# A decoder layer on one core: an eighth chunk of the last projection in seven products, with weight sums made in DRAM by accumulating DMAs

## The chip, the core and the metric

The kernel runs on one core of a Trainium2 chip. Time is the device time of one execution in microseconds (us); a profiled execution also has a span, from its first instruction to its last. Engines are TensorE (PE in the profile; PEld are its weight loads), VectorE (DVE), ScalarE (ACT), GpSimd (POOL) and SyncE (SP). Each runs its own queue in the order in which the program names its instructions, and waits at an instruction until what it needs is there. DMAs are issued from the queues of SP, ACT or POOL.

## What is computed

A decoder layer for 256 tokens of width 1024 in fp32: a mixer (causal pooling beside block attention), cross-attention into 256 memory tokens, and a SwiGLU FFN of width 2816, each followed by a residual and a LayerNorm. Only the last part matters here:

```python
def swiglu(h, w_gate, w_up, w_down):
    return (jax.nn.silu(h @ w_gate) * (h @ w_up)) @ w_down
...
h = layer_norm(DEEPNORM_ALPHA * h + swiglu(h, w_gate[l], w_up[l], w_down[l]), ln3_g[l], ln3_b[l])
```

## The kernel before

**Products in halves.** A product of fp32 matrices is made from halves of both operands, a high part cast to fp32r (ScalarE) and the rest, the low part (VectorE), as three matmuls: high times high, high times low, low times high (`three`, L359). So every weight tile, 128 partitions by 1024 numbers (0.524 MB), is loaded raw, cast by ScalarE, and its low part made by VectorE.

**The weights' stream.** The class `Stream` holds all weights in one list in the order of use. `fetch_ahead` (L112) issues the loads from SP, with up to 7 raw tiles not yet split (pool "raw", 7 buffers). `prepare` (L148) splits a tile; `next` (L176) splits one more whenever TensorE is done with one, and keeps 8, later 10, split tiles ahead (`widen`, L108). `before(number, load)` puts another load in front of a tile's load.

**Gate and up.** The FFN's width is cut into 11 chunks of 256 (c = 0 to 10), whose weights are tiles w59 to w102, four for each chunk. `h2T` is the transposed input, in two tiles of the pool "a8": k = 0 to 3 and k = 4 to 7. A pass of the loop at L997 runs chunk c through `proj_both` (L369): matmuls with high weights into four PSUM banks (L377), then with low weights (L383). The last three passes do this in groups of two k, a tile of weights at a time. Odd passes use the banks of `accbank`, even ones those of `bank`, four each. After a pass, `Gated.add` empties its banks (L963 ScalarE, L964 VectorE). In the next pass `multiply` (L968, L969) and `split` (L971) follow, after the pass's second and fourth step: the gated values are cast to high and low parts (L429, L430).

**Down.** The second product, with w_down, takes the chunks in the order `DOWN = (1, 2, 0, 3, ..., 10)`. A chunk multiplies a 256 x 256 block of gated values with a 256 x 1024 block of weights. Seen as 2 x 2 blocks that is eight products of 128 x 128 by 128 x 512, or seven with Strassen's scheme in Winograd's form: sums of quarters of both operands are multiplied, and the seven results are shared among the outputs. Chunks 1 to 7 (`SEVEN`) take seven products (`seven`, L1033), 21 matmuls; chunk 0 takes eight (`eight`, L1054), 24 matmuls; chunks 8, 9 and 10 (`LAST`) take eight too, ordered by output quarter (`pieces`, L1065), so that the last LayerNorm can begin on the first half. The products go to PSUM banks m1, m2, m3, m5 (`accbank`) and m7, m6, m4, m0 (`bank`). A chunk's first five products are in the order m1, m2, m3, m5, m7.

The sums of a seven-product chunk's weights are made on VectorE in `prepare_pair` (L122): four subtractions of 128 x 512 beside three low parts of 128 x 1024 and one of 128 x 512, in three steps for the chunk's three tiles. Those of its gated values are made in `split` (L977 to L984): four operations of 128 x 128 and a second cast and low part.

**Buffers of gated values.** A seven-product chunk takes a whole tile of the pool "a8" for its gated values and their sums (`gated_parts`, L912); of the others, the first two share one such tile (go0), the third takes two tiles of the pool "pr", the fourth half a tile of "a8". The pool "a8" has `A8_BUFS = 11` buffers (L33). A new tile of a pool takes over a buffer, and its first writer waits until the last reader of the buffer's former tile is done. `h2` (the residual, read at the end) and `h2T` are also tiles of "a8".

Of the kernel before, what the change touches and what calls it, by code (L numbers as in the profile page):

```python
# [23 lines left out]
FB = DFF // P  # L24
# [10 lines left out]
BUSY = 7  # L35


DOWN = (1, 2, 0, 3, 4, 5, 6, 7, 8, 9, 10)
SEVEN = (1, 2, 3, 4, 5, 6, 7)
LAST = DOWN[-3:]  # L40
ALL = slice(None)

# [3 lines left out]
def r32(t):  # L46
    return t.bitcast(F32)


class Stream:  # L50
# [71 lines left out]
    def prepare_pair(self, i, hi, lo):  # L122
        nc = self.nc
        first, step = self.pairs[i]
        self.fetch(first + 3, nc.sync)
        x, y, z = self.raws[first:first + 3]
        h = x.shape[2] // 2
        (x1, x2), (y1, y2), (z1, z2) = [(a[:, :, :h], a[:, :, h:]) for a in (x, y, z)]
        sub = nc.vector.tensor_sub

        if step == 0:
            own = self.corner[first] = self.own(first)
            nc.scalar.copy(own[:, 0:1, :], x1)
            nc.scalar.copy(hi, y)
            sub(z1, x2, x1)
            sub(z2, y2, x2)
            sub(own[:, 1:2, :], x1, r32(own[:, 0:1, :]))
            sub(x2, y2, z1)
            sub(lo, y, r32(hi))
        elif step == 1:  # L140
            nc.scalar.copy(hi, z)
            sub(x1, y1, x2)
            sub(lo, z, r32(hi))
        else:
            nc.scalar.copy(hi, x)
            sub(lo, x, r32(hi))
# [59 lines left out]
@with_exitstack  # L206
def decoder_layer(
    ctx: ExitStack, tc: tile.TileContext, x, x_t, mem_t, w_qkv, w_u, w_pool, w_out,
    ln1_g, ln1_b, w_xq, w_xk, w_xkv, w_xo, ln2_g, ln2_b, w_gu, w_down, ln3_g, ln3_b, out,
):  # L210
    nc = tc.nc
    cp = ctx.enter_context(tc.tile_pool(name="const", bufs=1))
# [20 lines left out]
    ws = Stream(nc, rp, wp)  # L233
# [5 lines left out]
    def rows(w, k0, c0, nk=1, width=D):  # L239
        return ws.add(w[k0 * P:(k0 + nk) * P, c0:c0 + width].rearrange("(k p) n -> p k n", p=P), 1)  # L240
# [20 lines left out]
    c_xq = [cols(w_xq, c) for c in range(4)]  # L261
    c_xo = [rows(w_xo, k, 0) for k in range(KD)]
    c_gu = [ws.add(w_gu[c], 4) for c in range(NFC)]
    c_dn = {}
    for c in DOWN:
        tiles = [w_down[k * P:(k + 1) * P, :].rearrange("(k p) n -> p k n", p=P) for k in (2 * c, 2 * c + 1)]
        c_dn[c] = ws.add_pair(*tiles) if c in SEVEN else [ws.add(w, 1)[0] for w in tiles]
    ws.own = lambda i: sp.tile([P, 2, 512], F32R, tag="pair", bufs=3, name=f"w{i}c")


# [1 line left out]
    class Both:  # L272
# [62 lines left out]
    ws.before(c_dn[LAST[0]][0], load_norm("g", 3, ln3_g))  # L335
    ws.before(c_dn[LAST[0]][1], load_norm("b", 3, ln3_b))

    ident = cp.tile([P, P], F32, name="ident")
    make_identity(nc, ident)
    ident_r = cp.tile([P, P], F32R, name="ident_r")  # L340
# [4 lines left out]
        out=tri[:, P:], in_=tri[:, P:], compare_op=OP.is_ge, fill=NEG, base=0,  # L345
# [6 lines left out]
    mhalf = cp.tile([P, 32], F32, name="mhalf")[:, 0:1]  # L352
# [16 lines left out]
    def proj_both(pss, numbers, yT, group=KD):  # L369

        for k0 in range(0, KD, group):
            for k in range(k0, k0 + group):
                hi, _ = ws.get(numbers, k)
                for b, ps in enumerate(pss):
                    nc.tensor.matmul(ps, hi[:, b * P:(b + 1) * P], yT.both(k), start=k == 0, stop=False,  # L377
                                     skip_group_check=True)
                yield
            for k in range(k0, k0 + group):  # L380
                _, lo = ws.parts_of(numbers, k)
                for b, ps in enumerate(pss):
                    nc.tensor.matmul(ps[:, S:], lo[:, b * P:(b + 1) * P], yT.pair(k)[0], start=False,  # L383
                                     stop=k == KD - 1, skip_group_check=True)
# [313 lines left out]
    class Norm:  # L698
# [9 lines left out]
        def add(self, c0, c1, acc):  # L708
            self.sum(c0, c1, acc)
            self.measure(c0, c1)  # L710
# [219 lines left out]
    def gated_pair(c, k, t):  # L930

        return pair(gT[c], ALL, 2 * k + t)
# [18 lines left out]
    class Gated:  # L951
# [19 lines left out]
        def split(self):  # L971
            gated_parts(self.c)
            hi, lo = gT[self.c]
            q = self.sums[0].rearrange("p f (t s) -> p (f t) s", t=T)
            split(hi[:, 0:4], lo[:, 0:4], q)
            if self.c in SEVEN:
                a11, a21, a12, a22 = [q[:, i] for i in range(4)]  # L977
                sums = sp.tile([P, 4, P], F32, name="sg", tag="pr", bufs=PR_BUFS)
                s1, s2, s3, s4 = [sums[:, i] for i in range(4)]
                nc.vector.tensor_add(s1, a21, a22)  # L980
                nc.vector.tensor_sub(s3, a11, a21)
                nc.vector.tensor_sub(s2, s1, a11)
                nc.vector.tensor_sub(s4, a12, s2)  # L983
                split(hi[:, 4:8], lo[:, 4:8], sums)  # L984

    first = [bank("pg") for t in range(T)]
# [37 lines left out]
    m = {n: accbank(f"m{n}") for n in (1, 2, 3, 5)}  # L1024
# [3 lines left out]
    def into(n, y, w, cols=ALL, ps=None):  # L1028

        three((m[n] if ps is None else ps)[:, cols], y, w, n not in begun, True, True)  # L1030
        begun.add(n)
# [17 lines left out]
            ws.used += 1  # L1049
            ws.next()  # L1050

    QUARTERS = {2: (0, 0, 512), 3: (0, 512, D), 4: (1, 0, 512), 0: (1, 512, D)}

    def eight(c):  # L1054

        for k, number in enumerate(c_dn[c]):
# [42 lines left out]
    lower, upper = slice(0, 512), slice(512, D)  # L1099
    norms = [Norm(3, t, h2[:, t, :]) for t in range(T)]  # L1100
# [10 lines left out]
    m1, u2, u3 = [shared_sum(name) for name in ("m1", "u2", "u3")]  # L1111
# [3 lines left out]
    with_residual(0, upper, m[5])  # L1115
    nc.vector.tensor_add(u3, m[7], u2)
    with_residual(1, upper, m[5])
    nc.vector.tensor_add(norms[0].r[:, upper], norms[0].r[:, upper], u2)
    nc.vector.tensor_add(norms[1].r[:, upper], norms[1].r[:, upper], u3)
# [15 lines left out]
    for half in HALVES:  # L1135
# [28 lines left out]


_INS = ["x", "x_t", "mem_t", "w_qkv", "w_u", "w_pool", "w_out", "ln1_g", "ln1_b", "w_xq", "w_xk",
        "w_xkv", "w_xo", "ln2_g", "ln2_b", "w_gu", "w_down", "ln3_g", "ln3_b"]


# [42 lines left out]
```

## Time and profile before

| | us |
|---|---|
| median of 3 runs | 377.5 (377.05 to 377.51) |
| the profiled execution | 376.66 |
| its span | 374.9 |
| TensorE busy | 368.5 |
| VectorE busy | 306.8 |
| ScalarE busy | 204.1 |
| GpSimd busy | 19.6 |

In a list of instructions in order of time, a line gives start, duration, engine, line of the kernel, operation, output and inputs with shapes, and in brackets how long the engine idled before it and what ended that. In a table by stretches, a line gives from:to, its length, then for PE, PEld, DVE, ACT and POOL the busy time and number of instructions, the TensorE clock that was granted (1.00 is full), the DMA engines' mean busy share, and GB/s. The chain of waits is the work that ended last, followed back from the end.

### The profile page before, as it was taken

The page shows a single profiled execution, that of the slowest core. Times are in us where ns is not written, and L with a number is a line of the kernel's source. Part 1 is how long each engine was busy: PE and PEld are TensorE (multiplying, and loading weights), DVE is VectorE, ACT ScalarE, POOL GpSimd, SP SyncE. Part 2 cuts the span into 40 slices and gives each one's busy share as a digit, 9 for nine tenths or more (in the row PEclk, how much of TensorE's full clock was granted, in tenths as well). Part 3 has the DMA queues.
Part 4 walks back from the last instruction along what each step waited for, and adds up shares of the span by engine and source line. Part 5 has one row for each costly group of instructions (what it writes and reads, how often), then busy time and mean ns, then how long its engine had stood idle before and what let it go on. Part 6 is the DMA issues. An engine that isn't in the chain of part 4 may idle for free.

```text
span 374.9 us, 5582 instructions
## 1 busy us (share of the span) xinstructions
PE 368.5 (98%) x2061; PEld 317.6 (85%) x2061; DVE 306.8 (82%) x498; ACT 204.1 (54%) x330; POOL 19.6 (5%) x27
## 2 busy tenths in 40 slices
PE   9999999999999999999999999999999999999994
PEld 8997878787888889998888888888898888888883
DVE  6768799975599677865889688888888999999984
ACT  6746677644154635644237675567665675546510
POOL 1000033400020000000100000000000000000021
PEclk9999999999999999999999999999999999999998
DMA  8997784668508963343106958665554453375202
GB/s 274 415 416 270 222 282 124 214 214 292 169 0 281 387 210 133 113 156 123 60 2 221 326 184 278 226 219 176 173 180 170 152 170 113 119 275 162 64 0 112
DMA packets 20891, 71.93 MB, mean 192 GB/s; under 512 B 2304, under 2 KB 3072, under 8 KB 20736
## 3 DMA queue, kind: packets, MB, share of 16 engines
q1 hardware_dynamic: 20432, 71.12, 54.3%
q10 hardware_dynamic: 432, 0.46, 0.4%
q8 instruction: 16, 0.26, 0.3%
q14 instruction: 11, 0.09, 0.1%
HBM read 70.52 MB, written 1.05 MB: 191 GB/s over the span
## 4 chain that ended last, share of the span: by engine, by line
PE 97%; DMA 1%; DVE 1%; ACT 0%; issue 0%; POOLq 0%; ACTq 0%
PE pg L377 19%; PE pg L383 10%; PE pqk L483 6%; PE m L362 5%; PE m L364 5%; PE m L363 5%; PE acc L362 4%; PE acc L363 4%; PE acc L364 4%; PE pxk L377 4%; PE pxq L377 4%; PE pxq L383 2%; PE pu L377 2%; PE pxk L383 2%; PE xv L362 2%; PE xv L364 2%
## 5 line engine op out<-in xcount | busy, mean ns | idle before, releaser
L725 POOL TENSOR_TENSOR rs<-rs,mhalf 128x1 f32<-128x1 f32 x6 | 5.0, 830 | 291.2 <-DVE rs L724 291.2
L429 ACT CAST g<-sg 128x512 fp32r<-128x512 f32 x14 | 8.7, 621 | 19.1 <-DVE sg L983 12.4
L430 DVE TENSOR_TENSOR g<-sg,g 128x512 fp32r<-128x512 f32 x14 | 9.7, 692 | 8.9 <-ACT g L429 8.9
L964 DVE TENSOR_TENSOR sg<-pg,sg 128x256 f32<-128x256 f32 x40 | 14.1, 416 | 0.0
L963 ACT COPY sg<-pg 128x256 f32<-128x256 f32 x40 | 11.8, 379 | 2.1 <-PE pg L383 2.1
L968 ACT ACTIVATE sg<-sg 128x512 f32<-128x512 f32 x10 | 6.3, 635 | 12.1 <-DVE sg L964 12.0
L520 ACT ACTIVATE xpr<-xs,mx 128x256 f32<-128x256 f32 x8 | 3.7, 470 | 14.3 <-DVE mx L531 14.3
L520 ACT ACTIVATE pr<-pr,mx 128x128 f32<-128x128 f32 (+1 forms) x16 | 7.1, 445 | 7.6 <-DVE mx L551 7.6
L429 ACT CAST h2T<-tp 128x512 fp32r<-128x512 f32 x4 | 2.3, 586 | 12.9 <-PE tp L440 12.9
L730 DVE SCALAR_TENSOR_TENSOR r<-r,mv,gb 128x512 f32<-128x512 f32 (+2 forms) x12 | 8.3, 722 | 0.0
L717 DVE BATCH_NORM_STATS2 st<-r 128x6 f32<-128x512 f32 (+1 forms) x12 | 8.0, 670 | 0.3
L969 DVE TENSOR_TENSOR sg<-sg 128x512 f32<-128x512 f32 x10 | 6.9, 692 | 0.8
L596 POOL TENSOR_TENSOR win<-upad 128x542 f32<-128x542 f32 x2 | 4.0, 1998 | 56.9 <-DVE upad L627 56.9
L525 DVE RECIPROCAL sm<-sm 128x2 f32<-128x2 f32 x12 | 2.0, 166 | 6.0 <-ACT xpr L520 4.5
L835 PE MATMUL xs<-xkTh,xq 128*128 128x256 f32 x32 | 6.4, 282 | 0.0
L429 ACT CAST h1T<-tp 128x512 fp32r<-128x512 f32 x4 | 2.4, 588 | 7.2 <-PE tp L440 7.2
L735 DVE SCALAR_TENSOR_TENSOR h<-r,rs,gb 128x512 f32<-128x512 f32 x8 | 5.7, 746 | 0.1
L596 POOL TENSOR_TENSOR win<-win 128x269 f32<-128x269 f32 (+3 forms) x4 | 5.8, 1446 | 0.2
L635 ACT CAST xkTh<-pxk 128x256 fp32r<-128x256 f32 x8 | 2.6, 377 | 5.5 <-PE pxk L383 5.5
L637 DVE TENSOR_TENSOR xkl<-pxk,xkTh 128x256 f32<-128x256 f32 x8 | 3.0, 416 | 3.1 <-ACT xkTh L635 3.1
L835 PEld LDWEIGHTS xs<-xkTh,xq 128*128 128x128 f32 x32 | 5.2, 190 | 0.2
L170 ACT CAST w39h<-w39r 128x1024 fp32r<-128x1024 f32 x1 | 1.0, 1049 | 7.8 <-PE acc L364 7.8
(1157 smaller groups left out, 1294.8 us busy)
## 6 DMA issues: line engine op xcount, KB each, us to landing
gb<-in_ln_g SPq DMA_DIRECT2D x3, 512.0 KB, 6.0
gb<-in_ln_b SPq DMA_DIRECT2D x3, 512.0 KB, 7.5
wr<-in_w_qkv SPq DMA_DIRECT2D x5, 256.0 KB, 4.4
mr<-in_mem_t SPq DMA_DIRECT2D x1, 1024.0 KB, 11.4
xt<-in_x SPq DMA_DIRECT2D x1, 1024.0 KB, 7.8
xr<-in_x_t SPq DMA_DIRECT2D x3, 256.0 KB, 6.1
wr<-in_w_qkv SPq DMA_DIRECT2D x1, 512.0 KB, 6.0
w7r<-in_w_qkv SPq DMA_DIRECT2D x1, 512.0 KB, 6.9
```

The lines of the kernel that those rows point to most:

```text
L362: nc.tensor.matmul(ps, wa, ya, start=start, stop=False, skip_group_check=part)
L363: nc.tensor.matmul(ps, wa, yb, start=False, stop=False, skip_group_check=part)
L364: nc.tensor.matmul(ps, wb, ya, start=False, stop=stop, skip_group_check=part)
L377: nc.tensor.matmul(ps, hi[:, b * P:(b + 1) * P], yT.both(k), start=k == 0, stop=False, skip_group_check=True)
L383: nc.tensor.matmul(ps[:, S:], lo[:, b * P:(b + 1) * P], yT.pair(k)[0], start=False, stop=k == KD - 1, skip_group_check=True)
L429: nc.scalar.copy(h, ps)
L483: nc.tensor.matmul(qk[i][:, f, :], w[:, c * P:(c + 1) * P], y, start=k == 0 and f == 0 and w is hi and y is x_hi, stop=k == KD - 1 and w i ...
L520: nc.scalar.activation(dst[:, j, :], src[:, j, :], AF.Exp, bias=mx[:, j:j + 1], scale=sign, accum_out=sm[:, j:j + 1])
L596: nc.gpsimd.tensor_add(nxt[:, j:, 2 * n - 1:], cur[:, j:, 2 * n - 1:], cur[:, j:, n - 1:PADW + S - n])
L835: nc.tensor.matmul(ps[:, t, :], q[:, kk, t * P:(t + 1) * P], k[:, 2 * h + kk], start=n == 0, stop=q is q_lo and kk == 1, skip_group_check= ...
L963: nc.scalar.copy(y[:, f, :], ps[:, S:])
L964: nc.vector.tensor_add(y[:, f, :], ps[:, :S], y[:, f, :])
```

## The change

Chunk 8 becomes the eighth chunk of seven products; chunk 0 takes its place among the last three, so that `eight` goes away and nothing is preloaded into m0. The scheme's signs are changed so that all sums of weights are additions. For chunks 5 to 8 (`SUMMED`) the sums are no longer made on VectorE. The host lays the quarters of these chunks' weights out as a further input, `w_sum` (order: lower left, lower right, upper right, upper left). Two DMAs on SP copy pairs of quarters to DRAM scratch tensors `sum_z` and `sum_w` (2.1 MB each) during the passes of cross-attention and gate, and three accumulating DMAs on POOL, named in pass 3 of gate and up, add further quarters to them (2.1, 2.1 and 1.05 MB). In down such a chunk loads tiles y (two plain quarters), z and w (two sums each) and, for two chunks at a time, o (their upper left quarters), 14 tiles for the four chunks, each split as a plain tile. Nothing changes in the pools but the padding of a constant; `dynamic_dma_scratch_size` goes from 256 to 1024.

```diff
-DOWN = (1, 2, 0, 3, 4, 5, 6, 7, 8, 9, 10)
-SEVEN = (1, 2, 3, 4, 5, 6, 7)
+DOWN = (1, 2, 3, 4, 5, 6, 7, 8, 0, 9, 10)
+SEVEN = DOWN[:-3]
+SUMMED = (5, 6, 7, 8)
 LAST = DOWN[-3:]
...
+    dram = ctx.enter_context(tc.tile_pool(name="dram", bufs=1, space=bass.MemoryType.DRAM))
+    sum_z, sum_w = [dram.tile([P, 2, len(SUMMED), 512], F32, name=f"sum_{name}") for name in "zw"]
     c_dn = {}
     for c in DOWN:
...
+        if c in SUMMED:
+            j = SUMMED.index(c)
+            order = [("y", w_sum[:, 0:2, j, :]), ("z", sum_z[:, :, j, :]), ("w", sum_w[:, :, j, :])]
+            if j % 2 == 0:
+                order.append(("o", w_sum[:, 3, j:j + 2, :]))
+            c_dn[c] = {what: ws.add(src, 1)[0] for what, src in order}
...
+    ws.before(c_gu[1][0], lambda: nc.sync.dma_start(sum_z, w_sum[:, 1:3]))
+    ws.before(c_gu[2][0], lambda: nc.sync.dma_start(sum_w, w_sum[:, 0:2]))
+
+    def add_quarters():
+        def add(dst, src):
+            nc.gpsimd.dma_start(dst, src, accum_op=OP.add, max_dma_last_dim=8192)
+
+        add(sum_z, w_sum[:, 2:4])
+        add(sum_w, sum_z[:, 1:2].to_broadcast(list(sum_w.shape)))
+        add(sum_w[:, 0], w_sum[:, 1])
...
         if c == 3:
             ws.widen(late)
+            add_quarters()
...
+    def summed(c):
+
+        plan = {"y": ((c, 2, 2), (c, 3, 7)), "z": ((c, 7, 6), (c, 5, 4)), "w": ((c, 4, 3), (c, 6, 5)),
+                "o": ((c, 1, 0), (c + 1, 1, 0))}
+        for what, number in c_dn[c].items():
             ws.prepare(number + 1)
-            hi, lo = ws.tiles[number]
-            for n, (t, c0, c1) in QUARTERS.items():
-                into(n, gated_pair(c, k, t), (hi[:, 0, c0:c1], lo[:, 0, c0:c1]))
+            for half, (of, n, form) in enumerate(plan[what]):
+                into(n, pair(gT[of], ALL, form), tuple(a[:, half] for a in ws.tiles[number]))
+                yield
             ws.used += 1
             ws.next()
-            yield
...
         for c in DOWN[:-len(LAST)]:
-            yield from (seven if c in SEVEN else eight)(c)
+            yield from (summed if c in SUMMED else seven)(c)
...
-    add(norms[1], 768, D, m[0][:, 256:])
```

More of the change, by code (lines that the diff above doesn't have):

```diff
@@ L128, in prepare_pair @@
         (x1, x2), (y1, y2), (z1, z2) = [(a[:, :, :h], a[:, :, h:]) for a in (x, y, z)]
-        sub = nc.vector.tensor_sub
+        sub, add = nc.vector.tensor_sub, nc.vector.tensor_add
         if step == 0:
@@ L134, in prepare_pair @@
             nc.scalar.copy(hi, y)
-            sub(z1, x2, x1)
-            sub(z2, y2, x2)
+            add(z1, x2, x1)
+            add(z2, y2, x2)
             sub(own[:, 1:2, :], x1, r32(own[:, 0:1, :]))
-            sub(x2, y2, z1)
+            add(x2, y2, z1)
             sub(lo, y, r32(hi))
@@ L141, in prepare_pair @@
             nc.scalar.copy(hi, z)
-            sub(x1, y1, x2)
+            add(x1, y1, x2)
             sub(lo, z, r32(hi))
@@ L208, in decoder_layer @@
     ctx: ExitStack, tc: tile.TileContext, x, x_t, mem_t, w_qkv, w_u, w_pool, w_out,
-    ln1_g, ln1_b, w_xq, w_xk, w_xkv, w_xo, ln2_g, ln2_b, w_gu, w_down, ln3_g, ln3_b, out,
+    ln1_g, ln1_b, w_xq, w_xk, w_xkv, w_xo, ln2_g, ln2_b, w_gu, w_down, w_sum, ln3_g, ln3_b, out,
 ):
@@ L266, in decoder_layer @@
         tiles = [w_down[k * P:(k + 1) * P, :].rearrange("(k p) n -> p k n", p=P) for k in (2 * c, 2 * c + 1)]
-        c_dn[c] = ws.add_pair(*tiles) if c in SEVEN else [ws.add(w, 1)[0] for w in tiles]
+        if c in SUMMED:
[4 more added lines that the diff above has]
+            c_dn[c] = {what: ws.add(src, 1)[0] for what, src in order}
+        elif c in SEVEN:
+            c_dn[c] = ws.add_pair(*tiles)
+        else:
+            c_dn[c] = [ws.add(w, 1)[0] for w in tiles]
     ws.own = lambda i: sp.tile([P, 2, 512], F32R, tag="pair", bufs=3, name=f"w{i}c")
@@ L350, in decoder_layer @@
                    allow_small_or_imprecise_dtypes=True)
-    mhalf = cp.tile([P, 32], F32, name="mhalf")[:, 0:1]
+    mhalf = cp.tile([P, 96], F32, name="mhalf")[:, 0:1]
     nc.vector.memset(mhalf, -0.5)
@@ L979, in split @@
                 s1, s2, s3, s4 = [sums[:, i] for i in range(4)]
-                nc.vector.tensor_add(s1, a21, a22)
+                nc.vector.tensor_sub(s1, a21, a22)
                 nc.vector.tensor_sub(s3, a11, a21)
                 nc.vector.tensor_sub(s2, s1, a11)
-                nc.vector.tensor_sub(s4, a12, s2)
+                nc.vector.tensor_add(s4, a12, s2)
                 split(hi[:, 4:8], lo[:, 4:8], sums)
@@ L1050, in seven @@
             ws.next()
-    QUARTERS = {2: (0, 0, 512), 3: (0, 512, D), 4: (1, 0, 512), 0: (1, 512, D)}
-    def eight(c):
-        for k, number in enumerate(c_dn[c]):
+    def summed(c):
+        plan = {"y": ((c, 2, 2), (c, 3, 7)), "z": ((c, 7, 6), (c, 5, 4)), "w": ((c, 4, 3), (c, 6, 5)),
+                "o": ((c, 1, 0), (c + 1, 1, 0))}
+        for what, number in c_dn[c].items():
             ws.prepare(number + 1)
-            hi, lo = ws.tiles[number]
-            for n, (t, c0, c1) in QUARTERS.items():
-                into(n, gated_pair(c, k, t), (hi[:, 0, c0:c1], lo[:, 0, c0:c1]))
+            for half, (of, n, form) in enumerate(plan[what]):
+                into(n, pair(gT[of], ALL, form), tuple(a[:, half] for a in ws.tiles[number]))
+                yield
             ws.used += 1
             ws.next()
-            yield
+    QUARTERS = {2: (0, 0, 512), 3: (0, 512, D), 4: (1, 0, 512), 0: (1, 512, D)}
     def pieces():
@@ L1117, in decoder_layer @@
     with_residual(1, upper, m[5])
-    nc.vector.tensor_add(norms[0].r[:, upper], norms[0].r[:, upper], u2)
-    nc.vector.tensor_add(norms[1].r[:, upper], norms[1].r[:, upper], u3)
+    nc.vector.tensor_sub(norms[0].r[:, upper], norms[0].r[:, upper], u2)
+    nc.vector.tensor_sub(norms[1].r[:, upper], norms[1].r[:, upper], u3)
     with_residual(1, lower, u3)
-    add(norms[1], 768, D, m[0][:, 256:])
     rest = [sp.tile([P, CW], F32R, name=f"rest{i}", tag="pr", bufs=PR_BUFS) for i in range(2)]
@@ L1166 @@
 _INS = ["x", "x_t", "mem_t", "w_qkv", "w_u", "w_pool", "w_out", "ln1_g", "ln1_b", "w_xq", "w_xk",
-        "w_xkv", "w_xo", "ln2_g", "ln2_b", "w_gu", "w_down", "ln3_g", "ln3_b"]
+        "w_xkv", "w_xo", "ln2_g", "ln2_b", "w_gu", "w_down", "w_sum", "ln3_g", "ln3_b"]
 def kernel(**inputs):
@@ L1173 @@
     from concourse.bass_utils import run_bass_kernel_spmd
-    nc = bacc.Bacc("TRN2", target_bir_lowering=False, num_devices=1, dynamic_dma_scratch_size=256)
+    nc = bacc.Bacc("TRN2", target_bir_lowering=False, num_devices=1, dynamic_dma_scratch_size=1024)
     arrays, args = {}, []
@@ L1202 @@
     given["w_gu"] = np.concatenate([chunks(given["w_gate"]), chunks(given["w_up"])], axis=3)
+    quarters = given["w_down"].reshape(FB // 2, 2, P, 2, 512)[list(SUMMED)]
+    given["w_sum"] = np.stack([quarters[:, i, :, j].transpose(1, 0, 2) for i, j in ((1, 0), (1, 1), (0, 1), (0, 0))],
+                              axis=1)
     for name in _INS:
```

## The prediction

> **What bounds the kernel now.** First the page's span and busy times, then the chain that ended last, cut out where gate and up give way to down.
>
> ```profile
> span 374.9 us, 5582 instructions
> PE 368.5 (98%) x2061; PEld 317.6 (85%) x2061; DVE 306.8 (82%) x498; ACT 204.1 (54%) x330; POOL 19.6 (5%) x27
> ```
>
> ```profile
> 306.89 1.84 PE pg L377 x8
> 311.52 0.95 PE pg L383 x8
> 312.48 0.23 PE m L362
> 316.81 0.23 PE m L363
> ```
>
> TensorE is the bound, and at 312.48 down's first product (into m, L362) follows gate and up's last matmul without a gap. Nineteen matmuls of 128x512 start between 312.48 and 316.81: 4.33 / 19 = 0.228 us each. A matmul removed is worth that, as long as nothing makes TensorE wait. So the next view is the busy time in stretches.
>
> ```profile
> 290.00:298.00 8.00, 8.00 (x48) 6.99 (x47) 7.72 (x13) 5.25 (x10) 0.00 (x0) 1.00 0.56 190
> 298.00:306.00 8.00, 8.00 (x47) 7.00 (x46) 7.94 (x13) 4.05 (x8) 0.00 (x0) 1.00 0.31 90
> 306.00:314.00 8.00, 8.00 (x48) 7.03 (x47) 7.72 (x12) 5.94 (x11) 0.00 (x0) 1.00 0.49 177
> ```
>
> After the stretch come length, PE, PEld, DVE, ACT, POOL. VectorE is busy 7.72, 7.94 and 7.72 of 8 us just before down. It hides behind TensorE, with nothing to spare: whatever holds it up here is passed on.
>
> **The change, part by part.**
>
> *Matmuls.* Chunk 8 goes from eight products to seven: 3 x 0.228 = 0.68 us less on the path. Chunk 0 takes its place in the last pieces, same matmuls.
>
> *Chunk 8's gated values.* SEVEN now holds 8, so gated_parts(8) takes a whole tile of the pool "a8". Count its 11 buffers when chunk 8 is split, in pass c = 9: h2T has two, h2 one, go0 one, g1 to g7 seven. All live: passes 9 and 10 still read h2T, the end reads h2, down the rest. In before, chunk 8 went into the second half of go0 and needed none. The twelfth tile must wait for the first of the eleven to be read out, which is h2T's first half (k = 0 to 3). Pass 10 reads it last at k = 3, that is with w100. ScalarE casts into the tile first, and its queue is in order:
>
> ```profile
> 295.43 1.03 ACT L145 CAST w105h<-w103r 128x1024 fp32r<-128x1024 f32 x1
> 296.37 0.61 ACT L429 CAST go<-sg 128x512 fp32r<-128x512 f32 x1
> 296.89 0.61 ACT L133 CAST w106c<-w106r 128x512 fp32r<-128x512 f32 x1
> ```
>
> ```profile
> 303.94 2.00 PE L377 MATMUL pg<-h2T,w100h 128*128 128x512 f32 x8
> 305.78 1.12 PE L383 MATMUL pg<-h2T,w100l 128*128 128x256 f32 x8
> 306.73 2.00 PE L377 MATMUL pg<-h2T,w101h 128*128 128x512 f32 x8
> ```
>
> The cast now at 296.37 (go, chunk 8) would wait until the w100 matmuls end at 306.9. TensorE gets there unhindered: weights up to w105 are cast ahead of it in the queue, and pass 10's banks are emptied at 294. Behind the waiting cast stand w106 and all later weights, and the emptying of passes 9's and 10's banks; VectorE stops at the low part that follows.
>
> ```profile
> 284.43 0.69 DVE L430 TENSOR_TENSOR g<-sg,g 128x512 fp32r<-128x512 f32 x1
> 285.03 0.29 DVE L980 TENSOR_TENSOR sg<-sg 128x128 f32<-128x128 f32 x1
> 286.73 0.69 DVE L430 TENSOR_TENSOR g<-sg,g 128x512 fp32r<-128x512 f32 x1 [0.69 <-ACT g L429]
> 292.37 0.69 DVE L142 TENSOR_TENSOR w103r<-w104r,w103r 128x512 f32<-128x512 f32 x1
> 294.11 1.41 DVE L964 TENSOR_TENSOR sg<-pg,sg 128x256 f32<-128x256 f32 x4
> 297.64 0.68 DVE L430 TENSOR_TENSOR go<-sg,go 128x512 fp32r<-128x512 f32 x1
> 298.24 0.69 DVE L135 TENSOR_TENSOR w108r<-w106r 128x512 f32<-128x512 f32 x1
> 303.66 1.22 DVE L146 TENSOR_TENSOR w108l<-w106r,w108h 128x1024 fp32r<-128x1024 f32 x1
> 304.81 1.41 DVE L964 TENSOR_TENSOR sg<-pg,sg 128x256 f32<-128x256 f32 x4
> 307.19 1.23 DVE L172 TENSOR_TENSOR w109l<-w109r,w109h 128x1024 fp32r<-128x1024 f32 x1 [0.18 <-ACT w109h L170]
> 308.33 0.69 DVE L430 TENSOR_TENSOR go<-sg,go 128x512 fp32r<-128x512 f32 x1
> 308.94 1.22 DVE L172 TENSOR_TENSOR w110l<-w110r,w110h 128x1024 fp32r<-128x1024 f32 x1
> 310.07 0.69 DVE L135 TENSOR_TENSOR w113r<-w111r 128x512 f32<-128x512 f32 x1
> 313.62 1.41 DVE L964 TENSOR_TENSOR sg<-pg,sg 128x256 f32<-128x256 f32 x4
> ```
>
> Neighbours on VectorE follow each other closer than their durations, so I step by starts. ScalarE: 306.9 + 0.6 = 307.5. VectorE: low part 0.60 (284.43 to 285.03), 308.1; then, new for chunk 8, four sums and a second split, 285.03 to 286.73 + 0.60 = 2.30, 310.4; then down's second chunk, 298.24 to 304.81 = 6.57, 317.0. Only now L964 empties pass 9's banks, at 304.81 before. From it to pass 10's L964 went 8.81; in that stretch stood chunk 0's two tiles (1.14 + 1.13) and step 0 of the next (3.55). Now it is chunk 3's three tiles: 3.55, 1.74 (292.37 to 294.11) and 1.15 (303.66 to 304.81), 0.62 more. So pass 10's L964 starts at 317.0 + 9.43 = 326.4, against 313.62.
>
> TensorE finishes pass 10 at 312.48. Down's first four products write m1, m2, m3, m5, which are pass 9's banks; the first is free one addition after 317.0, at 317.4: a wait of 4.9 us, and 2.7 us of work. The fifth product, m7, needs pass 10's first bank, free at 326.4 + 0.4 = 326.8: a wait of up to 6.7. In before it ran at 312.48 + 12 x 0.228 = 315.2, with its bank free at 314.0. **Down runs 326.8 - 315.2 = 11.6 us late** from there. Chunks 2 and 3 are split by then, and chunk 4 near 336, before its turn at 326.8 + 3 x 0.68 + 2 x 4.8 = 338.4.
>
> *The clock.* TensorE never pauses that long in before; the nearest rows are after its last work.
>
> ```profile
> 370.15 0.91 PE L1156 MATMUL end<-r,diag 128*128 128x384 f32 x2 [1.46 <-ACT diag L1153]
> 371.50:372.00 0.50, 0.00 (x0) 0.00 (x0) 0.02 (x1) 0.07 (x1) 0.00 (x0) 1.00 0.00 0
> 372.50:372.75 0.25, 0.00 (x0) 0.00 (x0) 0.00 (x0) 0.00 (x0) 0.00 (x0) 0.62 1.03 401
> ```
>
> The granted clock (third from the end) falls from 1.00 in that 372.50 row, 1.5 us after TensorE's last work, and some 3.9 after dense work stopped at 368.7 (370.15 less the 1.46 of idling). Two waits of 4.9 and 6.7 us should bring it down. Lost time in the first stretch hides in the second wait. After the second, no row shows how soon the clock comes back: from nothing, if it does not fall, to twice 2.0. I take 2.0: half speed for as long as it took to fall, 3.9 us. [...]
>
> *Weights in down.* A chunk in sums costs VectorE 3.5 tiles of 1.14 (307.19 to 308.33) = 4.0 us instead of 6.57, while TensorE takes 21 x 0.228 = 4.8 for it. VectorE so gains on TensorE from chunk 5 on; it ends a late stretch early, and TensorE being the bound, that is worth nothing. Its DMA reads grow from 8 to 14 tiles for chunks 5 to 8.
>
> *Copies and accumulations.* Two copies of 2.1 MB join SP's queue ahead of w63 and w67; accumulations of 2.1, 2.1 and 1.05 MB go on POOL, which has nothing queued until 362.
>
> ```profile
> 153.21 0.33 SPq L102 DMA_DIRECT2D w63r<-in_w_gu  x1
> 171.97 0.33 SPq L102 DMA_DIRECT2D w67r<-in_w_gu  x1
> 362.12 0.92 POOL L725 TENSOR_TENSOR rs<-rs,mhalf 128x1 f32<-128x1 f32 x1 [170.69 <-DVE rs L724]
> 205.00:254.00 49.00, 49.00 (x285) 43.36 (x284) 39.26 (x65) 29.43 (x48) 0.00 (x0) 1.00 0.71 245
> 254.00:290.00 36.00, 36.00 (x216) 32.11 (x216) 30.95 (x50) 23.48 (x37) 0.00 (x0) 1.00 0.52 177
> ```
>
> 245 GB/s at share 0.71 make 345 at full share. The copies: 4.2 / 0.345 = 12 us, among loads cast only after 195; hidden. The accumulations start near 191 (362.12 - 170.69) and are due when down's fifth chunk is loaded, near 326. No row shows one: I bound it by 5.24 / 0.345 = 15 us of the DMA engines, if an addition costs what a load of its bytes costs, and four times that, 61. Free between 205 and 290: 49 x 0.29 + 36 x 0.48 = 31 us. Loads run a dozen tiles ahead of TensorE, so I take nothing, being nearer to the load's price; the upper end is a rival.
>
> In down a tile of 0.524 MB takes 0.524 / 0.345 = 1.5 us to load. Chunk 5 is loaded before chunk 4 is split, which by the steps above ends near 336; then 16 tiles and the two norm vectors (18 x 1.5 = 27 us) end near 363, and TensorE comes to the last tile near 369. The lead hides them; at 0.8 of that rate it would be gone.
>
> **Sum:** 11.6 + 2.0 - 0.7 = +12.9 us on the span: 387.8. The profiled execution took 376.66, 1.76 more than its span; the median of the three runs, 377.5, lies 0.84 above it. 387.8 + 1.76 + 0.84 = **390.4 us**.
>
> **The rivals.**
>
> *The clock stays up*: the wait alone, 388.4. For it: the 1.46 us pause at 368.7 left the clock at 1.00. Against it: the waits are three to five times as long.
>
> *Chunk 8 finds a buffer at once*, because a tile that I count as live has been read out. VectorE still has 2.30 + 0.62 more to do before pass 10's L964: the bank frees near 317.0 instead of 314.0, m7 waits 1.8, net +1.1: 378.6. Against it: the count of readers above.
>
> *Not slower*: chunk 8 finds its buffer at once and VectorE takes in the 2.9 us, so that pass 10's L964 starts by 314.8. That start decides; then only the three matmuls count: 377.5 - 0.7 = 376.8. Against it: VectorE idles 0.6 of the 24 us shown.
>
> *The accumulations crowd out weight loads* in gate and up. It decides above the 31 us that are free plus what a dozen tiles hold (6.3 / 0.345 = 18 us), at 49 us for the 5.24 MB; at the upper end of 61 it adds 12: 402. Against it: all three fit twice over at a load's price. [...]
>
> **How the numbers follow.** Forecast with the clock's fall 0.52; clock stays up 0.33; buffer at once 0.06; not slower 0.05; crowding 0.04. The range 386 to 394 spans the first two cases, with the clock term from none to twice its size and 2 us off the wait's chain, and leaves out the others and a little of these: about 0.8. A measurement tells about 0.2% (0.75 us) from no change. Faster by more 0.02 and within it 0.04, from the not-slower case, which lies at -0.7, and the low end of the buffer-at-once one; slower 0.94.
>
> **What would show it.** Right: ScalarE idle before the first cast of g8, released by a gate or up matmul, for about 10 us from 296; VectorE idle beside it; TensorE idle some 5 us before m1 and up to 7 before m7, released by L964; granted clock under 1 just behind; afterwards products without gaps to the end, and 2058 matmuls in all instead of 2061. Wrong: g8's cast at about 296 without a wait, or pass 9's L964 near 305. Gaps in gate and up released by DMA would be the crowding; gaps in chunks 5 to 8 released by DMA would mean I undercounted the loads in down.

## The result, and the profile after

| | before | after |
|---|---|---|
| median of 6 runs, us | 377.5 (376.77 to 377.71) | 390.58 (389.74 to 391.34) |
| the profiled execution | 376.66 | 389.74 |
| its span | 374.9 | 388.0 |

The change makes the kernel slower: the ratio is 1.035, with a 95% interval of 1.0335 to 1.0366. The forecast was 390.4.

Lines of the changed kernel are numbered some 24 higher: the casts and low parts of gated values, L429 and L430 before, are L453 and L454, the emptying of a pass's banks is L987 and L988, the three matmuls of `three` are L386 to L388. First the span and the busy times of the page of after:

```profile
span 388.0 us, 5600 instructions
PE 372.7 (96%) x2058; PEld 320.4 (83%) x2058; DVE 303.8 (78%) x490; ACT 207.7 (54%) x331; POOL 22.8 (6%) x30
```

Three matmuls fewer, as named, and 13.1 us more span. Where TensorE waited is told by its table of waits in after (total, times, longest):

```profile
PE m L386 <- DVE sg L988: 8.9, 2, 5.1
```

Two waits before products of down, both released by L988 on VectorE. The instructions of TensorE in after around them, then those of ScalarE and of VectorE:

```profile
306.20 1.12 PE L407 MATMUL pg<-h2T,w100l 128*128 128x256 f32 x8
...
311.79 1.11 PE L407 MATMUL pg<-h2T,w102l 128*128 128x256 f32 x8
318.02 0.77 PE L386 MATMUL m<-w103c,g 128*128 128x512 f32 x1 [5.12 <-DVE sg L988]
...
327.19 0.80 PE L386 MATMUL m<-w104h,g 128*128 128x512 f32 x1 [3.75 <-DVE sg L988]
```

```profile
291.19 1.04 ACT L171 CAST w102h<-w102r 128x1024 fp32r<-128x1024 f32 x1
...
300.01 1.03 ACT L146 CAST w105h<-w103r 128x1024 fp32r<-128x1024 f32 x1
307.35 0.62 ACT L453 CAST g<-sg 128x512 fp32r<-128x512 f32 x1 [6.31 <-PE pg L407]
```

```profile
308.01 0.69 DVE L454 TENSOR_TENSOR g<-sg,g 128x512 fp32r<-128x512 f32 x1 [5.71 <-ACT g L453]
...
317.46 1.41 DVE L988 TENSOR_TENSOR sg<-pg,sg 128x256 f32<-128x256 f32 x4
...
326.72 1.41 DVE L988 TENSOR_TENSOR sg<-pg,sg 128x256 f32<-128x256 f32 x4
```

Read them as one chain. ScalarE idles before the first cast of chunk 8's gated values until a matmul of gate and up releases it (307.35); it is the low group of w100, which ends at 307.3 (306.20 + 1.12). VectorE idles beside it, empties pass 9's banks at 317.46 and pass 10's at 326.72, and TensorE begins m1 and m7 half a microsecond after each.

One thing in the ScalarE rows was not in the forecast: the idle time is 6.31 us, not about 10 us. w105's cast ends at 301.0, where before it ended at 296.5: ScalarE already ran 4.6 us late (w102h is cast at 291.19, and the row of before, just below, says 286.61).

```profile
286.61 1.04 ACT L170 CAST w102h<-w102r 128x1024 fp32r<-128x1024 f32 x1
```

That lateness comes from earlier. These are stretches of gate and up, first of before, then of after (the last two columns are the DMA engines' busy share and GB/s):

```profile
205.00:220.00 15.00, 15.00 (x88) 13.18 (x87) 10.46 (x18) 7.57 (x13) 0.00 (x0) 1.00 0.86 310
220.00:235.00 15.00, 15.00 (x96) 13.64 (x95) 13.08 (x20) 10.76 (x16) 0.00 (x0) 1.00 0.64 211
```

```profile
205.00:220.00 15.00, 15.00 (x86) 13.09 (x85) 9.56 (x14) 7.87 (x12) 1.06 (x1) 1.00 1.04 312
220.00:235.00 15.00, 15.00 (x98) 13.69 (x97) 11.19 (x18) 8.95 (x13) 0.84 (x1) 1.00 1.02 315
```

The DMA engines are full for 30 us (shares of 1.04 and 1.02), and VectorE did 2.8 us less work in that time. So two candidates stood: the wait for the buffer, and the accumulations. By the trace of after alone they can't be parted.

### The profile page after: what moved, and what is told of

Its sections match the earlier page's. It is cut to its first block, busy times and chain, and to the rows that moved or that the text cites. A ratio compares the mean times of both kernels' runs of the same rounds, so it can differ in the third digit from the quotient of the medians.

```text
span 388.0 us, 5600 instructions
## 1 busy us (share of the span) xinstructions
PE 372.7 (96%) x2058; PEld 320.4 (83%) x2058; DVE 303.8 (78%) x490; ACT 207.7 (54%) x331; POOL 22.8 (6%) x30
## 3 DMA queue, kind: packets, MB, share of 16 engines
q0 software_dynamic: 688, 5.24, 6.6%
## 4 chain that ended last, share of the span: by engine, by line
PE 93%; DVE 4%; ACT 1%; issue 0%; POOLq 0%; ACTq 0%; DVEq 0%
PE pg L401 18%; PE pg L407 9%; PE pqk L507 6%; PE m L386 4%; PE m L388 4%; PE m L387 4%; PE acc L386 4%; PE acc L387 4%; PE acc L388 4%; PE pxq L401 4%; PE pxk L401 4%; PE pxq L407 2%; PE pu L401 2%; PE pxk L407 2%; PE xv L386 2%; PE xv L388 2%
## 5 line engine op out<-in xcount | busy, mean ns | idle before, releaser
L453 ACT CAST g<-sg 128x512 fp32r<-128x512 f32 x16 | 9.9, 620 | 25.9 <-DVE sg L1007 14.1
L454 DVE TENSOR_TENSOR g<-sg,g 128x512 fp32r<-128x512 f32 x16 | 11.1, 692 | 15.3 <-ACT g L453 15.3
L988 DVE TENSOR_TENSOR sg<-pg,sg 128x256 f32<-128x256 f32 x40 | 14.1, 413 | 0.0
L987 ACT COPY sg<-pg 128x256 f32<-128x256 f32 x40 | 11.8, 378 | 0.0
L453 ACT CAST h2T<-tp 128x512 fp32r<-128x512 f32 x4 | 2.3, 586 | 12.9 <-PE tp L464 12.9
L453 ACT CAST h1T<-tp 128x512 fp32r<-128x512 f32 x4 | 2.4, 588 | 7.2 <-PE tp L464 7.2
L386 PE MATMUL m<-w103c,g 128*128 128x512 f32 x1 | 0.8, 767 | 5.1 <-DVE sg L988 5.1
## 6 DMA issues: line engine op xcount, KB each, us to landing
sum_w<-sum_z POOLq DMA_DIRECT2D x1, 2048.0 KB, 18.2
mr<-in_mem_t SPq DMA_DIRECT2D x1, 1024.0 KB, 11.6
```

The lines of the kernel that those rows point to most:

```text
L386: nc.tensor.matmul(ps, wa, ya, start=start, stop=False, skip_group_check=part)
L453: nc.scalar.copy(h, ps)
L454: nc.vector.tensor_sub(l, ps, r32(h))
L987: nc.scalar.copy(y[:, f, :], ps[:, S:])
L988: nc.vector.tensor_add(y[:, f, :], ps[:, :S], y[:, f, :])
```

## The experiments

**The theory** was the forecast's: the time goes into the wait of chunk 8's gated values for a twelfth tile of a pool with eleven buffers. **The rival**: the accumulations hold up the loads of gate and up, and the wait is where that shows. The times are medians; the ratio to the kernel before has its 95% interval in brackets.

**1. The eighth chunk is chunk 10 instead of chunk 8.** By the time chunk 10 is split, pass 10 has read h2T.

```diff
-DOWN = (1, 2, 3, 4, 5, 6, 7, 8, 0, 9, 10)
-SUMMED = (5, 6, 7, 8)
+DOWN = (1, 2, 3, 4, 5, 6, 7, 10, 0, 8, 9)
+SUMMED = (5, 6, 7, 10)
...
-                "o": ((c, 1, 0), (c + 1, 1, 0))}
+                "o": ((c, 1, 0), (DOWN[DOWN.index(c) + 1], 1, 0))}
```

> The eighth chunk in seven products is chunk 10 instead of chunk 8, so that its whole tile of "a8" is asked for only after pass 10, when h2T is free; the sums in DRAM and the count of matmuls are as in the change. The wait for the twelfth tile as the cause: ScalarE doesn't wait before any split in pass 9, pass 10's first L988 starts near 314.3 (0.62 later than before for chunk 3's third tile, inside 1.2 us of slack), no gap before m1 or m7, and three matmuls fewer: 376.8 us, 0.7 under before. VectorE's extra work as the cause: m7 waits 1 to 2 us, 378 to 379. The DMAs (copies, accumulations, six more loads in down) as the cause: near the change, above 385.

382.79 us, 1.0149 [1.0121, 1.0178]. Most of the loss is gone, but 6 us more are left than the theory allowed. TensorE's waits in this kernel:

```profile
PE m L386 <- DVE sg L988: 3.2, 1, 3.2
```

One wait by the same releaser remains: VectorE comes late to pass 10's banks without any wait for a buffer.

**2. The wait alone.** The kernel before, in which chunk 8's gated values take a whole tile; nothing else of the change.

```diff
-        if c in SEVEN:
+        if c in SEVEN or c == 8:
```

> The kernel before, with one edit: chunk 8's gated values get a whole tile of "a8" of their own (the twelfth) instead of the second half of go0. No sums in DRAM, no further product, no further split. The wait as the cause: the cast of chunk 8 waits until 306.9, VectorE's low part ends near 308.1 instead of 298.2, pass 10's L964 comes 9.9 later, m7 about 8.7 late (its bank had 1.2 of slack); with 1.4 us of half clock behind it 387.6, without 386.2. VectorE's extra work or the DMAs as the cause: 377.5, as before.

388.67 us, 1.0302 [1.0287, 1.0317]: 11.6 us from one condition, 1.1 us above the expected 387.6. Its row on ScalarE:

```profile
307.68 0.62 ACT L429 CAST g<-sg 128x512 fp32r<-128x512 f32 x1 [10.46 <-PE pg L383]
```

Here the idle time is 10.46 us, as the forecast had it. The wait is shown to be a sufficient cause. By its profile the excess lies mostly in the clock: m7 began at 324.76, 9.7 us late where 8.7 were expected (0.75 of it TensorE already had before pass 10), and half speed lasted from there to 330.8, which costs 3.0 us and not 1.4.

**3. Twelve buffers** in the change; for the room, seven split weights ahead instead of eight.

```diff
-RAW_BUFS, W_BUFS, LATE_BUFS = 7, 8, 2
-A8_BUFS = 11
+RAW_BUFS, W_BUFS, LATE_BUFS = 7, 7, 2
+A8_BUFS = 12
```

> The change with 12 buffers in "a8"; their room comes from one buffer less for split weights (7 instead of 8, so 7 and later 9 tiles ahead). The wait as the cause: no wait before g8's cast; what stays is VectorE's 2.30 + 0.62 us more before pass 10's L988: m7 waits up to 1.8, 377.3 to 379, and no fall of the clock. The DMAs as the cause: above 385, as the change. If fewer split tiles ahead cost something by themselves, gaps before other products would show it.

383.36 us, 1.0176 [1.0153, 1.0199]: 7 us less than the change, but 5 more than expected. No cast of gated values waits for the w100 matmuls any more. TensorE now waits for a weight, which the missing buffer may explain, and once for VectorE, 2.8 us where up to 1.8 were expected, with a fall of the clock behind it (320.6 to 327.4) that was not:

```profile
PE m L386 <- DVE sg L988: 2.8, 1, 2.8
PE pg L387 <- DVE w62l L173: 2.3, 1, 2.3
```

**4. The DMAs alone.** The kernel before with the copies and accumulations of the change, whose results nothing reads.

```diff
+    ws.before(c_gu[1][0], lambda: nc.sync.dma_start(sum_z, w_sum[:, 1:3]))
+    ws.before(c_gu[2][0], lambda: nc.sync.dma_start(sum_w, w_sum[:, 0:2]))
...
         if c == 3:
             ws.widen(late)
+            add_quarters()
```

> The kernel before with the change's two copies and three accumulating DMAs added, at the same places and into the same scratch tensors, which nothing reads. The wait as the cause: 377.5 within 0.4, accumulations of 14, 18 and some 10 us from 191 on beside the weights, no gap on TensorE. The DMAs as the cause: most of the change's 13 us. A few gaps in gate and up, released by a load, would be a part of it.

382.39 us, 1.014 [1.0119, 1.0162]: 5.4 us, where the forecast took nothing. This is about what chunk 10 had left. The waits of ScalarE between 185 and 320 us, and VectorE's behind them:

```profile
ACT w70h L171 <- DMA w70r<-in_w_gu: 3.1, 1, 3.1
ACT w76h L171 <- DMA w76r<-in_w_gu: 2.9, 1, 2.9
ACT w80h L171 <- DMA w80r<-in_w_gu: 2.4, 1, 2.4
```

```profile
DVE w76l L173 <- ACT w76h L171: 2.7, 1, 2.7
DVE w80l L173 <- ACT w80h L171: 1.8, 1, 1.8
DVE w70l L173 <- ACT w70h L171: 1.8, 1, 1.8
```

In before none of these waits is there. The lists of DMA issues give the time from issue to landing, in before and then in this kernel:

```profile
w70r<-in_w_gu SPq DMA_DIRECT2D x1, 512.0 KB, 3.3
...
w76r<-in_w_gu SPq DMA_DIRECT2D x1, 512.0 KB, 6.3
```

```profile
w70r<-in_w_gu SPq DMA_DIRECT2D x1, 512.0 KB, 7.7
...
w76r<-in_w_gu SPq DMA_DIRECT2D x1, 512.0 KB, 19.0
```

Loads land two to three times as late (7.7 us for 3.3, 19.0 for 6.3). VectorE loses 6.3 us in the three rows above and gets back 1.9 of them where it waited anyway (for chunk 0's gated values, 2.77 us before, 0.92 here). It finds no other slack, so it carries the rest to pass 10's banks. With smaller delays it empties them 6.0 us later than in before (319.62 against 313.62), while TensorE came only 0.7 late, and TensorE waits there:

```profile
PE m L376 <- DVE sg L978: 4.2, 1, 4.2
```

Why there was no lead is in SyncE's and ScalarE's rows of before:

```profile
179.83 0.33 SPq L102 DMA_DIRECT2D w69r<-in_w_gu  x1
198.08 0.33 SPq L102 DMA_DIRECT2D w70r<-in_w_gu  x1
...
206.36 0.33 SPq L102 DMA_DIRECT2D w77r<-in_w_gu  x1
```

```profile
202.66 1.04 ACT L170 CAST w70h<-w70r 128x1024 fp32r<-128x1024 f32 x1
```

Between 179.83 and 198 SyncE issues no load (seven raw tiles, w63 to w69, are waiting to be split); then eight go out in 8 us, and ScalarE takes the first 4.6 us after its issue. The accumulations start at 192 and lie on exactly this place.

**5. Chunk 10 without accumulations and copies.**

```diff
-            order = [("y", w_sum[:, 0:2, j, :]), ("z", sum_z[:, :, j, :]), ("w", sum_w[:, :, j, :])]
+            order = [("y", w_sum[:, 0:2, j, :]), ("z", w_sum[:, 1:3, j, :]), ("w", w_sum[:, 0:2, j, :])]
...
-            add_quarters()
```

> Chunk 10 in seven products as in the first experiment, but nothing is added in DRAM and nothing copied there: the z and w tiles are loaded as plain quarters of in_w_sum, so the sums of the weights are left out of the products; the number and size of the loads in down stay. If the 5.4 us that the DMAs cost beside the kernel before (382.39 against 377) are what chunk 10 still lost, the time falls from 382.8 to 376.8 (376.3 to 377.4): three products less than the kernel before. If chunk 10 loses its time in down (more loads, the order of the chunks), it stays at 382 to 383.

376.53 us, 0.9985 [0.9976, 0.9995]. All of chunk 10's loss is gone, and most of what three matmuls are worth shows (0.5 of 0.68 us). Down itself costs nothing that shows.

**6. The same DMAs, meant for later, in ten pieces.**

```diff
+        if 4 <= c < 9:
+            add_quarters(c - 4)
```

> Chunk 10 in seven products with the whole computation, the accumulations cut into ten pieces of half a megabyte and issued two a pass in passes 4 to 8 instead of all in pass 3. Theory: what costs is a burst in which loads land 15 to 20 us after issue where ScalarE takes them 9 to 18 us after; two pieces a pass add some 5 us of the 16 engines to a pass of 10.7 us in which half of them was free, loads land within 10 us, VectorE no longer waits: 376.8 to 378.0. Rival: the bytes cost the same wherever they lie, VectorE having no time to spare in any pass: 381.5 to 383.

392.08 us, 1.0397 [1.0368, 1.0426]: 9 us more than experiment 1, outside both expectations. GpSimd's rows say why:

```profile
191.63 1.78 POOL L358 DMA_DIRECT2D sum_z<-in_w_sum  x2
...
215.05 0.78 POOL L358 DMA_DIRECT2D sum_w<-in_w_sum  x1 [2.28 <-DMA sum_w<-sum_z]
```

Nothing moved. GpSimd has no work in gate and up that would hold it, so it issues a DMA that the program names in pass 8 as soon as its queue comes to it (the last of the ten at 215.05 us). The ten pieces went out even faster than three large ones, several under way at a time, and w74 landed 23.8 us after issue (11.5 in the change). TensorE then waits for VectorE twice, 5.8 us in gate and up and 5.4 before m7.

**7. The three large ones named in pass 6.**

```diff
+        if c == 6:
             add_quarters()
```

> The first experiment with its three large accumulations issued in pass 6 instead of pass 3, where the kernel before uses about half of the DMA engines' time, not 0.7 to 0.86. If only the busy place was the fault: 377 to 378.5. If the size of the burst is (2 MB at a time, loads land 12 to 20 us after issue while ScalarE takes them 9 us after), VectorE idles as before or more: 381.5 to 385.

382.85 us, 1.0163 [1.0138, 1.0189], the same as experiment 1, and no test either, for the reason just seen: the first accumulation was issued at 192.06 in this kernel, at 191.37 in experiment 1.

**8. The change without its accumulations.** The edit of experiment 5 on the change itself.

> The change itself (chunk 8 in seven products, eleven buffers) without the copies and accumulations: z and w tiles are loaded as plain quarters of in_w_sum, so the weights' sums are left out. Theory: the delay by the DMAs and the wait for the buffer don't add up, since the wait ends at a fixed matmul (TensorE's last read of h2T's first half) whatever the delay before it: 388.5 to 390.5. If they add up: 385.2 (390.6 less the 5.4 measured for the DMAs alone).

391.34 us, 1.0376 [1.0352, 1.04]: not faster than the change, and 0.8 us above the expected range. ScalarE's wait:

```profile
307.73 0.62 ACT L451 CAST g<-sg 128x512 fp32r<-128x512 f32 x1 [10.51 <-PE pg L405]
```

Without accumulations ScalarE idles 10.51 us, with them 6.31, and both end at the same matmuls, at 307.73 and 307.35. Whatever held ScalarE up before that is swallowed: the accumulations, 5.4 us alone, add nothing to the change. The intervals of the two kernels overlap; between their profiled executions (391.55 and 389.74 us) most of the difference is the clock's: behind the second wait half speed lasted from 327.56 to 333.5 here and from 327.19 to 330.1 in the change, which makes 1.5 us. For the change itself the theory stands; the rival is a second cause, which shows only where the wait is gone.

**9. Five accumulations of a megabyte, one a pass, held back.** GpSimd first reads an element of the gated values that the pass has split, and its queue waits for it.

```diff
-            add_quarters()
...
             left.split()
+            if 4 <= c < 9:
+                nc.gpsimd.tensor_tensor(spare[:, 1:2], r32(gT[c - 1][0])[:, 0, 0:1], mhalf, op=OP.add)
+                add_quarters(c - 4)
```

> The two runs that were to move the accumulations did not move them: GpSimd issued them at 191 to 215 us again, as soon as its queue was free, and ten pieces in flight together held the loads longer still. Here GpSimd first reads an element of the gated chunk that the pass has just split, so that five accumulations of a megabyte start in passes 4 to 8, one a pass. Theory of the burst: some 5 us of the 16 engines (25 us for all) come on a pass of 10.7 us in which half was free, loads land in 6 to 11 us where ScalarE takes the fourth load of a pass 12 us after issue, VectorE doesn't idle: 376.4 to 378.0. Rival, the bytes cost the same anywhere: 381.5 to 383.

376.99 us, 1.0001 [0.9991, 1.001]. No wait of TensorE for VectorE is left in gate and up and down.

**10. The three large ones held back to pass 6** by the same read.

```diff
-            add_quarters()
...
             left.split()
+            if c == 6:
+                nc.gpsimd.tensor_tensor(spare[:, 1:2], r32(gT[c - 1][0])[:, 0, 0:1], mhalf, op=OP.add)
+                add_quarters()
```

> The three large accumulations as they are in the change, but held by such a read until pass 6 (about 245 us). If the place alone decides (0.5 of the DMA engines' time is free there): 376.5 to 378. If the size of the burst decides: loads land 12 to 20 us after issue, ScalarE takes them 12 to 18 us after, VectorE idles 3 to 6 us in all: 380 to 383.

376.67 us, 0.999 [0.9981, 0.9999]. This is the fastest kernel here that makes the weights' sums, a tenth of a per cent below the kernel before. GpSimd's rows in it:

```profile
262.52 0.69 POOL L1034 TENSOR_TENSOR mhalf<-g,mhalf 128x1 f32<-128x1 f32 x1 [71.00 <-ACT g L454]
263.17 1.35 POOL L356 DMA_DIRECT2D sum_z<-in_w_sum  x1
278.25 1.06 POOL L356 DMA_DIRECT2D sum_w<-sum_z  x1 [13.73 <-DMA sum_z<-in_w_sum]
296.97 0.83 POOL L356 DMA_DIRECT2D sum_w<-in_w_sum  x1 [17.66 <-DMA sum_w<-sum_z]
```

The accumulations take as long as in the change (the first two land after 14.7 and 18.4 us, there after 14.0 and 18.2), but start 71 us later. So for these three it was the place, not the size of the burst. Loads are held up here too, but they have a lead: w100 is issued at 266.99, lands 10.7 us later (3.6 in before) and is cast at 278.20, half a microsecond on.

**11. Chunk 10 with the copies, without accumulations.** The edit is experiment 1's kernel less the call of `add_quarters`.

> Chunk 10 with the two copies of 2 MB on SyncE's queue but none of the accumulations (so the z and w tiles hold plain quarters, and the weights' sums are left out). If the accumulations alone hold up the loads of gate and up: 376.5 to 377.1, as without copies. If the copies do (they are issued at 153 and 167 us, and w63 lands 11 us after issue): 379 to 382.8.

376.08 us, 0.998 [0.9971, 0.9989]. The copies cost nothing; the 5.4 us are the accumulations'. Three matmuls are 0.68 us, and 0.8 came out. Against this kernel and experiment 5 the accumulations cost chunk 10's version some 6.3 us (1.0149 against 0.998 and 0.9985).

**12. Chunk 8 with twelve buffers, the accumulations held to pass 6**: experiment 3's edit with experiment 10's.

> Chunk 8 in seven products as in the change, with twelve buffers of the pool a8 (and seven of the weights' pairs instead of eight, for the room) and the three accumulations held until pass 6. If the two causes found are all (the wait for the twelfth buffer, the accumulations beside the dense loads at 198 to 215 us), both are gone and it stands at 376.5 to 377.5, with up to 2 us more if the seventh weight buffer's wait before w62 (2.3 us with the accumulations early) stays: up to 379.5. If chunk 8 has a cost of its own (chunks 0, 9 and 10 together have to be ready, the work of VectorE late in gate and up), 380 or more.

384.63 us, 1.018 [1.015, 1.021]: the two known causes are not all. Moving the accumulations brought nothing here (experiment 3: 1.0176). TensorE's waits in this kernel, and VectorE's emptying of the banks of passes 8, 9 and 10:

```profile
PE m L387 <- DVE sg L989: 2.6, 1, 2.6
PE pg L388 <- DVE w62l L173: 2.3, 1, 2.3
```

```profile
298.96 1.41 DVE L989 TENSOR_TENSOR sg<-pg,sg 128x256 f32<-128x256 f32 x4
...
312.50 1.41 DVE L989 TENSOR_TENSOR sg<-pg,sg 128x256 f32<-128x256 f32 x4
...
321.91 1.41 DVE L989 TENSOR_TENSOR sg<-pg,sg 128x256 f32<-128x256 f32 x4
```

Two losses of about the same size are in it. First, TensorE waits 2.3 us for w62, a weight that has no wait in before, and runs at half speed from 196.7 to 200.2; from there to the end of gate and up it is 4.5 us late, and VectorE with it. This comes long before the accumulations (267 us) and chunk 8. The room that the twelfth buffer took from the split weights is the likely cause, though seven weight buffers were not run alone. Second, chunk 8 has a cost of its own. In before the three rows stand at 294.11, 304.81 and 313.62, so here VectorE is 4.85, 7.69 and 8.29 us late: it loses 2.84 us between the first two (chunk 8's four sums and second split, 2.30 in the forecast, and the rest by other steps of tiles that fall there), and 0.60 between the others (0.62 in the forecast). The bank's slack takes up some of it; m7 waits 2.6 us, and half speed follows from 323.0 to 326.4. Experiment 3 shows the same 2.84 and 0.60. So in these two kernels chunk 8 in seven products costs more than the 0.7 us of three matmuls even though it finds a free buffer.

## Why the prediction was right, point by point

- **The wait for the twelfth tile** was right. L988 was forecast at 317.0 and 326.4 and came at 317.46 and 326.72; down's fifth product (m7) ran at 327.19, and its row of before is at 315.06: 12.1 us late, for 11.6. Of this, 0.42 us is older than the wait: the low group of w100 starts at 306.20, at 305.78 before, and TensorE waits for nothing in gate and up in either kernel. The parts were right too: without chunk 8's own work m7 came at 324.76 (experiment 2), with it at 327.56 (experiment 8), 2.8 us for the forecast 2.30 + 0.62. That experiment 2 as a whole costs 11.6 us as well is a coincidence: it lacks this work and contains a loss by the clock.
- **The wait's length on ScalarE** was right only without the accumulations (10.46 and 10.51 in experiments 2 and 8). In the change it was 6.31, because the accumulations had made ScalarE and VectorE late already. Its end, which sets the time, was forecast at 306.9 and came at 307.35, 307.68 and 307.73.
- **The clock** was taken at 2.0 us. The stretches of after behind the two waits (granted clock third from the end):

```profile
314.00:316.00 2.00, 0.00 (x0) 0.00 (x0) 2.00 (x3) 0.76 (x1) 0.00 (x0) 1.00 0.00 0
316.00:317.00 1.00, 0.00 (x0) 0.00 (x0) 0.97 (x2) 1.00 (x5) 0.00 (x0) 0.71 0.58 127
317.00:323.00 6.00, 4.98 (x12) 3.81 (x12) 5.89 (x11) 4.03 (x7) 0.00 (x0) 0.50 0.47 154
323.00:324.00 1.00, 0.44 (x2) 0.00 (x0) 1.00 (x3) 0.00 (x0) 0.00 (x0) 0.87 0.00 0
324.00:326.50 2.50, 0.00 (x0) 0.00 (x0) 2.47 (x3) 2.00 (x5) 0.00 (x0) 1.00 0.26 70
326.50:327.00 0.50, 0.00 (x0) 0.00 (x0) 0.50 (x2) 0.50 (x2) 0.00 (x0) 0.67 0.97 201
327.00:330.00 3.00, 2.81 (x7) 2.23 (x8) 3.00 (x8) 1.63 (x3) 0.00 (x0) 0.50 0.74 254
330.00:331.00 1.00, 1.00 (x6) 0.82 (x5) 1.00 (x2) 0.00 (x0) 0.00 (x0) 0.96 0.03 12
```

  It fell to 0.50 in both, as forecast; the loss in the first hid in the second wait, as forecast; behind the second, half speed lasted 2.9 us (327.19 to 330.1), seven matmuls at 0.43 instead of 0.228, 1.4 us. The fall was right and the size 0.6 too large in this execution. In experiments 2 and 8, behind the same wait, it was 3.0 us, so 2.0 lies between what the same wait cost in different executions.
- **The sum**: 12.1 + 1.4 - 0.7 = 12.8 of the 13.1 us measured on the span. I don't place the remaining 0.3. That the forecast came within 0.2 us of the median is partly luck. Two misses cancel, 0.5 too little for the wait and 0.6 too much for the clock. And the 0.84 us that it added from the profiled execution to the median was taken from before; after has the same 0.84 by chance, for another reason: its profiled execution is the fastest of the six, with a mean granted clock of 0.983, and the other five have 0.980 or 0.981.
- **"So I take nothing" for the accumulations was wrong as a judgement of cost**, though it changed no number of this result. Alone they cost 5.4 us, and in chunk 10's version some 6.3; in the change the wait hides them. The step that failed is the count of what is free: 31 us of the DMA engines between 205 and 290, and "a dozen tiles" of lead. The supply was taken over 85 us, and the accumulations ran in the 44 us from 191.8 to 235.3. The second and third, 3.1 of the 5.24 MB, lie behind 206, where before left 15 x 0.14 + 15 x 0.36 = 7.5 us; and the lead was taken at its average, at a place where the stream has none. The rival "crowding" asked for 49 us of DMA work before it would cost anything. The profile of after has for the accumulating queue (packets, MB, share of 16 engines):

```profile
q0 software_dynamic: 688, 5.24, 6.6%
```

  That is 0.066 x 388 = 25.6 us, less than the 31 and far less than the 49, and it costs. It is 1.7 times the 15 of a load's price.
- **Weights in down**: right. TensorE waits for no load there, and experiment 5 loses nothing to them.
- **The rival "chunk 8 finds a buffer at once"** was priced at a wait of 1.8 us and no fall of the clock. Experiments 3 and 12, where the buffer is free, show 2.8 and 2.6 us and a fall behind it.

## What to carry to other kernels

When an edit takes one more tile of a pool, count the tiles that are live at that moment and name the reader that frees the first. Here the wait ended there whatever came earlier (307.35, 307.68 and 307.73 us in the change and experiments 2 and 8), and it hid another cost, the accumulations' 5.4 us alone, that came out as soon as the wait was removed. Weigh added DMA traffic against the free share and the lead of the loads in the stretch where it runs (7.5 us here, behind 206), not against the sum of a phase (31 us). Named in pass 6, on a queue with nothing else to do, the first accumulation was issued at 192.06 us, when the queue reached it, and with a value of that pass to read first at 263.17 us (experiments 7 and 10). So give the queue something of the pass to wait for, and look at the start in the trace before a result is read as a test of the place.

## What the runs showed of the hardware

In slices of a quarter of a microsecond the clock granted in the trace of after is 1.00 or 0.50, apart from the slices in which it changes, so a mean between the two tells the moment. In the change these moments are 316.4, 323.3, 326.7 and 330.1 us (0.71, 0.87, 0.67 and 0.96 in the rows above), in experiment 2 317.2, 320.6, 324.0 and 330.8, in experiment 12 196.74, 200.16, 323.04 and 326.44. The gaps are 3.4 us or a multiple of it; 196.74 and 323.04, 126.3 us apart, are 37 steps of 3.41. In the change the clock falls once more at 384.7, behind TensorE's last work, 54.6 us or 16 steps after 330.1. So in these three traces the moments stand on a grid of 3.41 us, through work and waits alike. Waits of the same length did not cost the clock alike: before w62 TensorE waits 2.3 us in experiments 3 and 12, and the clock stays at 1.00 in the first and falls in the second, 0.9 us after the work has begun again. And half speed behind a long wait did not last equally long: 2.9 us behind the second wait of the change, 5.2 behind the first (318.02 to 323.3), 6.1 and 5.9 behind the second wait of experiments 2 and 8.

An accumulating DMA of 2.1 MB took 14 to 18 us to land at either place, from 192 us, where the loads of before take up to 0.86 of the DMA engines, and from 263 us, where they take about 0.5, and it held loads up at both: w76 landed 19.0 us after issue in experiment 4 (6.3 in before), w109 16.5 us in experiment 10 (5.7 in before). What differed is how soon ScalarE wanted those loads: in before it casts w70 4.6 us after its issue (198.08 to 202.66), and w100 11.2 us after (266.89 to 278.12).
